# RMSNorm with repeated rows on one core: the second group's first load in two transfers

## The chip, the cores and the metric

The kernel runs on one core of one Trainium2 chip. The metric is the device time of one execution in microseconds (us); lower is better. The time before is the median of three runs.

## The reference

```
x: (8, 512, 2048) float32     gamma: (2048,) float32
x_rep  = repeat(x, 2, axis=1)                       # each row twice: (8, 1024, 2048)
rms    = sqrt(mean(x_rep ** 2, over the last axis) + 1e-6)
out    = x_rep / rms * gamma                        # float32
```

Each of the 4,096 input rows of 8 KB is normalized, multiplied by gamma and written out twice. The input has 33.6 MB and the output 67.1 MB; there is no matrix product.

## The kernel before

One tile `y` in SBUF holds 24 rows of 2048 numbers in each of the 128 partitions, as three areas of eight rows: `first` (rows 0 to 7), `second` (8 to 15) and `third` (16 to 23). The input is cut into four loads of 8.39 MB. Each brings eight rows to each partition, 64 KB that lie together in DRAM. The output is cut into eight stores of 8.39 MB: four rows of each partition, each row twice.

The schedule is written out by hand (`manual_schedule`): every engine carries out its instructions in the order of the program, and waits by semaphores only for the data or the space that it needs. The function `four` does two loads and four stores, and it is called twice, so there are two groups. All eight-row loads (line 50) and all stores (line 53) are issued by SP on one DMA queue (q1 in the profile). The small loads of gamma are issued by ScalarE on its queue (q10).

In a group the order is as follows.

1. Load n goes to rows 4 to 11 (`first + K`): the upper half of `first` and the lower half of `second`. Load n + 1 goes to `third`. In the first group the constants come between the two: gamma, its broadcast to all partitions by GpSimd, and epsilon.
2. For load n's rows 0 to 3, two at a time: ScalarE sums the squares of each row (line 63) and takes the root (line 67). VectorE takes the reciprocal (line 73) and multiplies each row by it and by gamma (line 75) into every second row of `first`. ScalarE and VectorE copy those rows to the places beside them (line 82), and store (n, 0) sends `first`.
3. The same for load n's rows 4 to 7 within `second`, and store (n, 1).
4. ScalarE sums the squares of the eight rows of load n + 1. Its first four rows are scaled from `third` into `first`, which needs store (n, 0) to have read it; they are copied, and store (n + 1, 0) sends them. The last four are spread within `third`, and store (n + 1, 1) sends them.

The second group's first load, load 2, needs rows 4 to 11 free. Of these, rows 4 to 7 are read by store (1, 0) and rows 8 to 11 by store (0, 1). Its second load, load 3, needs `third` free, which store (1, 1) reads. On SP the order of issue is: load 0, load 1, stores (0, 0), (0, 1), (1, 0), (1, 1), load 2, load 3, stores (2, 0), (2, 1), (3, 0), (3, 1).

Gamma comes in one DMA with G = 16 pieces of C = 125 numbers, and in E = 3 more of 16 numbers each; GpSimd spreads the two parts by two broadcasts (lines 132 and 136). The pieces are staged in rows 0 to 2 of `y` in partition 0.

Of the kernel before, what the change touches and what calls it, by code (L numbers as in the profile page):

```python
# [1 line left out]

# [4 lines left out]


@with_exitstack
def kernel(  # L10
    ctx: ExitStack,
    tc: tile.TileContext,
    x: bass.AP,
    gamma: bass.AP,
    out: bass.AP,
):
    nc = tc.nc
    P = nc.NUM_PARTITIONS
    f32 = mybir.dt.float32
    Act = mybir.ActivationFunctionType  # L20
    Alu = mybir.AluOpType

    B, S, D = x.shape
    Bo, So, Do = out.shape
    R = So // S
    assert R == 2 and D == Do and B == Bo and So == S * R
    eps = 1e-6
    inv_d = 1.0 / float(D)


    K = 4
    N = B * S
    ntiles = N // (P * K)
    assert N % (P * K) == 0 and ntiles == 8
    H = 2
    x_t = x.rearrange("b s d -> (b s) d").rearrange("(n p k) d -> n p k d", p=P, k=H * K)
    out_t = out.rearrange("b s d -> (b s) d").rearrange("(n p h j) d -> n h p (j d)", p=P, h=H, j=K * R)

    singles = ctx.enter_context(tc.tile_pool(name="singles", bufs=1))
    rows = ctx.enter_context(tc.tile_pool(name="rows", bufs=1))  # L40
    junk = ctx.enter_context(tc.tile_pool(name="junk", bufs=1, space=bass.MemoryType.PSUM))
    small = ctx.enter_context(tc.tile_pool(name="small", bufs=4))

    y = rows.tile([P, 3 * K * R, D], f32, name="y")
    first, second, third = 0, K * R, 2 * K * R

    def load(n, at):
        nc.sync.dma_start(out=y[:, at : at + H * K, :], in_=x_t[n])  # L50

    def store(n, h, to):
        nc.sync.dma_start(
            out=out_t[n, h], in_=y[:, to : to + K * R, :].rearrange("p j d -> p (j d)")
        )

    def squares(at, rows):

        n = len(rows)
        ss = small.tile([P, n], f32, name=f"ss{n}")  # L60
        for c, k in enumerate(rows):
            sq = junk.tile([P, D], f32, name="sq")
            nc.scalar.activation(  # L63
                out=sq[:], in_=y[:, at + k, :], func=Act.Square, accum_out=ss[:, c : c + 1]
            )
        rms = small.tile([P, n], f32, name=f"rms{n}")
        nc.scalar.activation(out=rms[:], in_=ss[:], func=Act.Sqrt, scale=inv_d, bias=eps_t[:])  # L67
        return rms

    def scale(at, to, rows, rms):  # L70
        n = len(rows)
        rstd = small.tile([P, n], f32, name=f"rstd{n}")
        nc.vector.reciprocal(out=rstd[:], in_=rms[:])  # L73
        for c, k in enumerate(rows):
            nc.vector.scalar_tensor_tensor(  # L75
                out=y[:, to + R * k, :], in0=y[:, at + k, :], scalar=rstd[:, c : c + 1],
                in1=gamma_b[:], op0=Alu.mult, op1=Alu.mult,
            )

    def repeat(to, k0, k1, copy):  # L80
        y_r = y[:, to + R * k0 : to + R * k1, :].rearrange("p (k r) d -> p k r d", r=R)
        copy(out=y_r[:, :, 1, :], in_=y_r[:, :, 0, :])  # L82

    ctx.enter_context(tc.manual_schedule())

    half = K // 2
    up, down = list(range(K)), list(range(K - 1, -1, -1))

    def four(n, constants, step):


        load(n, first + K)
        constants()
        load(n + 1, third)
        for rows in (up[:half], up[half:]):
            scale(first + K, first, rows, squares(first + K, rows))
        repeat(first, 0, half, nc.scalar.copy)
        repeat(first, half, K, nc.vector.tensor_copy)
        store(n, 0, first)
        scale(second, second, down, squares(second, down))  # L100
        repeat(second, half, K, nc.scalar.copy)
        for k in range(0, half, step):
            repeat(second, k, k + step, nc.vector.tensor_copy)
        store(n, 1, second)
        roots = [squares(third + h * K, up) for h in range(H)]
        scale(third, first, up, roots[0])
        repeat(first, 0, half, nc.scalar.copy)
        repeat(first, half, K, nc.scalar.copy)
        store(n + 1, 0, first)
        scale(third + K, third, up, roots[1])  # L110
        repeat(third, 0, K, nc.scalar.copy)
        store(n + 1, 1, third)

    gamma_b = singles.tile([P, D], f32, name="gamma_b")
    G, E = 16, 3
    C = D // G - E
    gamma_s = y[0:1, 0:2, :].rearrange("p k (c d) -> p (k c) d", c=G // 2)
    gamma_t = y[0:1, 2, :]
    eps_t = singles.tile([P, 1], f32, name="eps_t")

    def constants():
        nc.scalar.dma_start(
            out=gamma_s[0:1, :, :C],
            in_=gamma[: G * C].rearrange("(p c d) -> p c d", p=1, c=G),
        )
        for c in range(E):
            at = G * C + c * G
            nc.scalar.dma_start(
                out=gamma_t[0:1, c * G : (c + 1) * G],
                in_=gamma[at : at + G].partition_broadcast(1),  # L130
            )
        nc.gpsimd.partition_broadcast(  # L132
            out_ap=gamma_b[:, : G * C].rearrange("p (c d) -> p c d", c=G),
            in_ap=gamma_s[0:1, :, :C],
        )
        nc.gpsimd.partition_broadcast(out_ap=gamma_b[:, G * C :], in_ap=gamma_t[0:1, : E * G])  # L136
        nc.vector.memset(eps_t, eps)  # L137

        root = singles.tile([P, 1], f32, name="root")[:]
        nc.scalar.activation(out=root, in_=eps_t[:], func=Act.Sqrt)  # L140

    four(0, constants, half)
    four(2, lambda: None, 1)


# [1 line left out]
_INS = ['x', 'gamma']  # L147
_OUTS = [((8, 1024, 2048), 'float32')]


# [23 lines left out]
```

## Time and profile before

| | |
|---|---|
| median of 3 runs | 238.07 us (238.01 to 238.34) |
| profiled execution | 238.07 us, span 236.2 us |
| busy: ScalarE / VectorE / GpSimd | 110.2 / 84.5 / 2.8 us |
| HBM read / written | 33.56 / 67.11 MB, 426 GB/s over the span |
| ScalarE idle until a load landed | 70.4 us in two waits |
| a row's sum of squares (line 63, ScalarE) | 1878 ns |
| a row's scaling (line 75, VectorE) | 2349 ns |
| SP's issue of a load (line 50) | 340 to 425 ns |
| issue to landing: loads / stores (median) | 31.4 / 24.8 us |

The span runs from the first to the last instruction; the rest of the time lies around it. Times in the profile are counted from the span's start. A wait "A <- B" is idle time of A that B's end released. The DMA row has the mean busy share of the 16 DMA engines in each fortieth of the span, in tenths. The queue lines give packets, MB, and the share of the 16 engines' time that the packets took. In the chain of work, the columns are start, duration, and what filled it.

### The profile page before, as it was taken

How to read it: one execution, taken by the hardware profiler on the slowest of the kernel's cores; microseconds unless marked ns; L12 is line 12 of the kernel's file. 1: busy time of each engine (PE TensorE's matmuls, PEld its weight loads, DVE VectorE, ACT ScalarE, POOL GpSimd, SP SyncE). 2: the span in 40 equal slices, each digit the busy share in tenths (PEclk: the TensorE clock that was granted, in tenths of full speed). 3: DMA queues.
4: the chain of work that ended last, by engine and by line, in shares of the span. 5: the costliest groups of instructions: out<-in, count | busy, mean ns of one | idle time of the engine just before them, and what ended most of it. 6: DMA issues, size and time to landing. Idle time of an engine off the chain costs nothing.

```text
span 236.2 us, 226 instructions
## 1 busy us (share of the span) xinstructions
DVE 84.5 (36%) x48; ACT 110.2 (47%) x86; POOL 2.8 (1%) x6
## 2 busy tenths in 40 slices
DVE  0000396594699500000000007928919992000000
ACT  2001989479998470000000049991999957400000
POOL 0110000000000000000000000000000000000000
DMA  9898989989898989989898998989898998989894
GB/s 355 356 533 355 510 377 422 466 366 522 355 533 356 533 355 422 466 377 510 355 533 355 488 400 355 533 355 533 355 533 355 488 399 355 533 355 533 355 533 178
DMA packets 1767, 100.68 MB, mean 426 GB/s; under 512 B 230, under 2 KB 230, under 8 KB 230
## 3 DMA queue, kind: packets, MB, share of 16 engines
q1 hardware_dynamic: 1728, 100.66, 98.7%
q10 hardware_dynamic: 38, 0.01, 0.0%
q14 instruction: 1, 0.01, 0.0%
HBM read 33.56 MB, written 67.11 MB: 426 GB/s over the span
## 4 chain that ended last, share of the span: by engine, by line
DMA 45%; ACT 26%; DVE 12%; issue 2%; DVEq 0%
DMA y<-in_x_dram 26%; DMA out_dram<-y 20%; ACT sq L63 15%; DVE y L75 12%; ACT y L82 11%; ACT rms L67 1%; DVE rstd L73 0%; DVEq L75 0%
## 5 line engine op out<-in xcount | busy, mean ns | idle before, releaser
L63 ACT ACTIVATE sq<-y 128x2048 f32<-128x2048 f32 x32 | 60.1, 1878 | 71.1 <-DMA y<-in_x_dram 70.4
L75 DVE SCALAR_TENSOR_TENSOR y<-y,rstd,gamma_b 128x2048 f32<-128x2048 f32 x32 | 73.8, 2349 | 1.6 <-DMA out_dram<-y 1.0
L82 ACT COPY y<-y 128x4096 f32<-128x4096 f32 (+1 forms) x10 | 42.6, 4283 | 19.1 <-DVE y L75 18.3
L73 DVE RECIPROCAL rstd<-rms 128x4 f32<-128x4 f32 (+1 forms) x10 | 1.7, 170 | 109.2 <-ACT rms L67 109.2
L82 DVE COPY y<-y 128x4096 f32<-128x4096 f32 (+1 forms) x5 | 9.2, 1865 | 0.1
L63 ACT ACTIVATION_READ_ACCUMULATOR sq<-y 128x1 f32 x32 | 6.0, 186 | 0.0
L67 ACT ACTIVATE rms<-ss,eps_t 128x4 f32<-128x4 f32 (+1 forms) x10 | 3.0, 297 | 0.3
L140 ACT ACT_TABLE_LOAD x1 | 1.3, 1283 | 2.6 <-issue 2.6
L132 POOL PARTITION_BROADCAST gamma_b<-y x1 | 2.2, 2243 | 10.2 <-DMA y<-in_gamma_dram 10.2
L136 POOL PARTITION_BROADCAST gamma_b<-y x1 | 0.3, 323 | 10.1 <-DMA y<-in_gamma_dram 10.1
L137 DVE MEMSET eps_t<- 128x1 f32 x1 | 0.1, 59 | 0.8 <-PEq L158 0.8
L140 ACT ACTIVATE root<-eps_t 128x1 f32<-128x1 f32 x1 | 0.2, 203 | 0.0
L158 POOL MEMSET const-bfloat16-1.0<- 128x1 bf16 x1 | 0.1, 102 | 0.0
L158 POOL MEMSET const-float32-0.0<- 128x1 f32 x1 | 0.1, 99 | 0.2 <-issue 0.2
L158 POOL MEMSET const-uint8-127<- 128x1 uint8 x1 | 0.1, 101 | 0.0
L158 POOL MEMSET const-float32-1.0<- 128x1 f32 x1 | 0.1, 98 | 0.0
## 6 DMA issues: line engine op xcount, KB each, us to landing
out_dram<-y SPq DMA_DIRECT2D x8, 24.8
y<-in_x_dram SPq DMA_DIRECT2D x4, 31.4
y<-in_gamma_dram ACTq DMA_DIRECT2D x3, 0.1 KB
y<-in_gamma_dram ACTq DMA_DIRECT2D x1, 7.8 KB, 9.8
```

What stands on the lines that cost most here:

```text
L63: nc.scalar.activation(out=sq[:], in_=y[:, at + k, :], func=Act.Square, accum_out=ss[:, c : c + 1])
L67: nc.scalar.activation(out=rms[:], in_=ss[:], func=Act.Sqrt, scale=inv_d, bias=eps_t[:])
L73: nc.vector.reciprocal(out=rstd[:], in_=rms[:])
L75: nc.vector.scalar_tensor_tensor(out=y[:, to + R * k, :], in0=y[:, at + k, :], scalar=rstd[:, c : c + 1], in1=gamma_b[:], op0=Alu.mult, op ...
L82: copy(out=y_r[:, :, 1, :], in_=y_r[:, :, 0, :])
L132: nc.gpsimd.partition_broadcast(out_ap=gamma_b[:, : G * C].rearrange("p (c d) -> p c d", c=G), in_ap=gamma_s[0:1, :, :C],)
L136: nc.gpsimd.partition_broadcast(out_ap=gamma_b[:, G * C :], in_ap=gamma_t[0:1, : E * G])
L137: nc.vector.memset(eps_t, eps)
L140: nc.scalar.activation(out=root, in_=eps_t[:], func=Act.Sqrt)
L158: nc = _bacc.Bacc("TRN2", target_bir_lowering=False, num_devices=1)
```

## The change

`load` gets a number of parts and issues one DMA for each, cut along the rows of each partition. `four` passes it on for its first load: the first group has one part as before, and the second group has H = 2. Load 2 so becomes two DMAs of 4.19 MB, rows 0 to 3 and 4 to 7 of each partition, 32 KB that lie together in DRAM for each. Gamma comes as 16 pieces of 126 numbers and two DMAs of 16 numbers instead of three.

```
-    def load(n, at):
-        nc.sync.dma_start(out=y[:, at : at + H * K, :], in_=x_t[n])
+    def load(n, at, parts=1):
+        w = H * K // parts
+        for k in range(0, H * K, w):
+            nc.sync.dma_start(out=y[:, at + k : at + k + w, :], in_=x_t[n][:, k : k + w, :])
...
-    def four(n, constants, step):
+    def four(n, constants, step, parts):
...
-        load(n, first + K)
+        load(n, first + K, parts)
...
-    G, E = 16, 3
+    G, E = 16, 2
...
-    four(0, constants, half)
-    four(2, lambda: None, 1)
+    four(0, constants, half, 1)
+    four(2, lambda: None, 1, H)
```

## The prediction

> **What bounds the kernel now.** I began with the page, because its share of DMA time says whether any engine can matter at all.
>
> ```profile
> span 236.2 us, 226 instructions
> ...
> DVE 84.5 (36%) x48; ACT 110.2 (47%) x86; POOL 2.8 (1%) x6
> ...
> DMA  9898989989898989989898998989898998989894
> ...
> q1 hardware_dynamic: 1728, 100.66, 98.7%
> ...
> DMA 45%; ACT 26%; DVE 12%; issue 2%; DVEq 0%
> ```
>
> The loads and stores all go through SP's queue (q1), and its packets fill 98.7% of the time of the 16 DMA engines. No slice of the span has a hole. VectorE and ScalarE are busy 36% and 47%. The chain (last line) puts 38% on ACT and DVE all the same. It runs from wait to wait, and does not know that a store issued after a computation then stands behind other transfers. So I set the chain in order of time beside SP's own waits.
>
> ```profile
> 76.17 23.86 DMA out_dram<-y
> 100.03 0.02 issue
> 100.04 38.78 DMA y<-in_x_dram
> 138.82 0.02 issue
> 138.85 2.01 ACT sq L63 x2
> ```
>
> ```profile
> SPq L53 <- DVE y L82: 84.1, 4, 35.2
> SPq L53 <- ACT y L82: 60.9, 4, 19.9
> SPq L50 <- DMA out_dram<-y: 31.9, 2, 19.3
> ```
>
> The second group's first load (load 2) is issued at 100.04 us and lands after 38.78 us. One transfer of 8.39 MB fills the engines for only some 19.3 us, so half of the 38.78 us is queueing behind the store ahead of it. To see whether the queue ever runs dry I read the trace's single DMA packet records (start, duration, size). Each of the 12 transfers is 128 packets of 64 KB, eight on each engine: 1,536 in all, of which 1,367 took 2.418 us, and the next begins 2.414 us after the one before. From the first packet of a transfer to the first of the next it is 19.318 or 19.319 us in 8 of 11 cases, which is 8 x 2.414 plus 0.007 for the semaphore write. The other three are 19.917 (the opening load), 19.354, and 19.739 (the last store of group one to load 2).
>
> So the profiled time adds up thus: the first packet starts at 1.74 us; 12 x 19.319 = 231.83; extra 1.43 (0.60 in the opening load, 0.42 at the turn from store to load, 0.04, and the rest the engines' offset from each other); last packet ends at 235.0; 1.2 to the end of the span; 1.87 around it. That is 238.07, and the median of the three runs is 238.07 too, so nothing needs rescaling. Only 1.43 us of the whole isn't bytes at full rate.
>
> The tightest point for computation is the first store of group two:
>
> ```profile
> 152.94 2.29 DVE L82 COPY y<-y 128x4096 f32<-128x4096 f32 x1
> ...
> 155.30 48.29 SPq L53 DMA_DIRECT2D out_dram<-y  x4
> ```
>
> It is issued at 155.30 us, when the copy at line 82 is done. Its first packet starts at 157.34, right behind load 3's, with no gap. The opening load needed 1.02 us from issue (0.72) to first packet (1.74), so this store had 157.34 - 155.30 - 1.02 = 1.0 us to spare. Small, but positive: no time is lost there.
>
> **The change part by part.**
>
> *The split of load 2, what it moves.* The first half fills y rows 4 to 7, which store (1, 0) reads, so it waits for the same landing as before and is issued at 100.04. The second half fills rows 8 to 11, free since store (0, 1) landed long before, and follows at once. Half a transfer is 9.66 us, so the first half lands at about 138.8 - 9.7 = 129.1 instead of 138.8. The squares, scaling and copies of rows 0 to 3 need nothing else and move up by 9.7 us. ScalarE reaches row 4 at 151.6 - 9.7 = 141.9, after the second half has landed (138.9): no new wait. It finishes the second four rows' copy at 168.4 - 9.7 = 158.7, and load 3 lands at 158.2, so that isn't waited for either. The first store is issued at 145.6 instead of 155.3. Its spare time grows from 1.0 to 10.7 us, and its packets still start at 157.3, because the queue is in order and load 3 stands ahead. Gain on the path: 0. The stall doesn't vanish but goes on: the scaling into `first` for load 3's rows has to wait until that store has read them, at 177.53 now:
>
> ```profile
> 155.30 22.23 DMA out_dram<-y
> 177.53 0.03 issue
> 177.56 0.05 DVEq L75
> 177.61 0.04 issue
> 177.65 7.62 DVE y L75 x4
> ```
>
> That moment is set by the queue and stays. From there the last two stores are issued where they were, or up to 3 us earlier for the third (ScalarE is free sooner), and those already had cover: the fourth's issue is at 203.3 and its packets start at 215.3.
>
> *The split, what it adds on SP.* One DMA instruction, 0.34 us by its row (340 to 425 ns at line 50). Behind it on SP stands load 3, which waits for the landing of store (1, 1) at 119.7; SP is idle from 100.4 to then, so it costs 0. Without that cover load 3 would be issued 0.34 us later, and it has until 138.0 before its packets' turn. Nobody waits for the added instruction but the rows of the second half, and those are 9.7 us off. POOL's and ACT's queues are not passed.
>
> *The split, what it adds on the DMA engines, which is the path.* Each engine carries 16 packets of 32 KB instead of 8 of 64 KB, and one more semaphore write. No row has 32 KB. The nearest are 64 KB at 2.418 us and the 8 KB instruction fetch in mid run at 0.309 us: the slope is 2.109 us over 57,344 bytes, and what remains at zero bytes is 0.008 us per packet. Eight more packets are 0.06 us, with the semaphore write 0.07. Low end: the records overlap by 4 ns, so 8 x 0.004 + 0.007 = 0.04; below nothing only if the turn from store to load (0.42) shrinks with smaller first packets, which would give -0.35. High end: the slowest 8 KB fetch, ahead of the program, took 0.512 us, 0.21 over its bytes; 8 x 0.21 = 1.7 us. I take 0.05, since 32 KB back to back in one queue is nearest to the 64 KB row and to the fetch in mid run.
>
> *Does a new transfer have a start-up of its own?* The trace has one load directly behind another, at 21 us: the boundary shows no stretched packet on any engine, and at the full queue's other boundaries the price is 0.007 us. The Trainium skill's "DMA: Bandwidth & Descriptors" (section "Anatomy of one DMA") gives a fixed cost of about 2 us for each DMA, most of it the wait for the write's receipt; if that were paid in line here, the estimate would be 240.1 us. The same page's "Rules for kernel authors" says that transfers under way together share the same 16 engines and serialize, so that splitting one (over partitions, in its wording) is not worth it. The first figure doesn't fit the 0.007 us of the boundaries, where the receipt is waited for beside the next transfer's bytes.
>
> *Gamma.* One issue on ACT's queue (213 to 671 ns) and two small packets (data and semaphore, 11 and 9 ns on one engine) go; the main piece has rows of 504 B instead of 500. ScalarE then idles until 22.67 us in any case. The second broadcast at line 136 ends at 23.3, some 2 to 5 us earlier with one small DMA less in line, and VectorE first needs gamma_b at 27.3: covered by 4 us. Worth at most 0.02 us on one engine: 0.
>
> Sum: 238.07 + 0.05 = 238.12 us.
>
> **The rivals.**
>
> *The halves don't chain (slower).* The second half starts as the opening load did, whose first packets took 2.83 to 3.52 us in place of 2.418, some 0.8 more in the mean. Place: the engines at about 128 us. Time: 238.07 + 0.05 + 0.8 = 238.9. For it: load 2 already lies behind the one costly turn (0.42). Against: the two loads at 21 us chain without it. It decides from a gap of 0.43 us on.
>
> *Small packets are dear (slower).* At the high end above, 239.8; it passes 0.2% from 0.054 us a packet on. Against: 8 KB in 0.309 us leaves 0.008.
>
> *Work done earlier fills holes (faster).* If all 1.43 us that aren't bytes went, 236.6. But they lie at the opening and at 118 us, ahead of every instruction that moves. Only the 0.42 can be touched: 237.7, still within the bound. More than that would need the first store to starve in some runs, and in the profiled one it has 1.0 us.
>
> *The change doesn't take hold.* The squares wait for both halves (one wait for the whole buffer). Then ScalarE starts at 138.9 as now, and the time is 238.1 by the same DMA sum.
>
> **How the numbers follow.** 0.2% of 238.07 is 0.48 us, about what a measurement of this kernel tells from no change (its three runs lie 0.33 apart). Forecast, 238.12: 0.70; not taking hold, also no change: 0.10. Halves not chaining: 0.08; dear packets: 0.06. Faster by over 0.48: 0.06. So faster 0.06, same 0.80, slower 0.14. The range goes from 237.7 (the turn's 0.42 saved) to 238.7, which takes in a boundary gap of 0.6 us and leaves out the dear packets.
>
> **What would show it.** Right: q1 with 1872 packets (144 more), the chain's first group-two square at about 129.2, SP's first group-two store issued near 145.6, q1's share still at 98% or more, and first packets of successive stores 19.319 us apart. Wrong: a gap or stretched packets at about 128 us; 32 KB packets over 1.27 us; VectorE's resumption not at 177.6; or ScalarE still starting at 138.9 (taking hold). The forecast fails if the engines' full rate depends on the packets' size or order, which the trace has only for 64 KB.

## The result and the profile after

The change makes the kernel slower: 239.38 us (median of 6, 239.2 to 239.53) against 238.09 us (median of 6, 238.0 to 238.98) for the kernel before. The ratio is 1.0045, 95% interval 1.0031 to 1.0058. The prediction was 238.12 us, "same" with a chance of 0.80, and its range ended at 238.7.

The profiled execution took 239.53 us, with a span of 237.7. The page of the changed kernel, in the lines that answer to those shown before:

```profile
span 237.7 us, 225 instructions
...
DVE 84.5 (36%) x48; ACT 110.5 (47%) x86; POOL 2.8 (1%) x6
...
DMA  9898989899998989898999999899898989899994
...
q1 hardware_dynamic: 1872, 100.66, 98.5%
```

The page shows almost nothing. The queue is as full as before and has the 144 extra packets of the split; the engines' busy times are the same. A share of 98.5% of a longer span does not say that the packets ran at full rate: a stretched packet counts as busy. The chain of work in order of time shows where the two executions part:

```profile
100.12 29.39 DMA y<-in_x_dram
129.51 0.02 issue
129.53 2.01 ACT sq L65 x2
...
145.99 32.95 DMA out_dram<-y
178.93 0.03 issue
178.96 0.05 DVEq L77
179.01 0.04 issue
179.06 0.18 DVE y L77
```

The first half of load 2 lands at 129.5 us and the first store of group two is issued at 145.99, both as planned (129.2 and 145.6). But that store lands at 178.93 instead of 177.53, and VectorE, which waits for it, resumes at 179.06 instead of 177.65. The forecast had named this moment as one that stays. So by then the DMA engines had lost 1.4 us, and single packets show where.

The DMA view of a window of 6 us (154 to 160) cuts it into 40 slices of 0.15 us; in so narrow a window the row marks the slices in which packets begin. Before the change:

```profile
DMA  0000009990000000000000999000000000000099
...
DMA packets 60, 2.88 MB, mean 481 GB/s; under 512 B 16, under 2 KB 16, under 8 KB 16
```

After:

```profile
DMA  0000009990090000000000000099999990090000
...
DMA packets 48, 2.10 MB, mean 350 GB/s; under 512 B 16, under 2 KB 16, under 8 KB 16
```

The first marks in both rows, from 154.9 us, are the last packets of load 3, the eighth on each engine. Before, the store's first packets begin 16 slices on, at 157.3. After, they begin at 158.0 to 159.3, spread out and late. The trace's single packet records give the size: load 3's last packets took 2.77 to 3.61 us on all 16 engines in place of 2.418 (2.418 to 2.427 before). All earlier packets of load 3 were at full rate, save for the one engine that an instruction fetch held up.

In what follows, "lost" is the time from the start of one packet to the start of the next on the same engine, over the 2.414 us of a packet at full rate (1.2095 for 32 KB), as a mean over the 16 engines. The changed kernel lost 0.84 us there, the kernel before 0.01. The sum over the whole execution, as mean of the engines' last packet ends: 235.72 us against 234.81, so 0.91 later. Of that, 0.83 lies at load 3's end, 0.07 at the turn before load 2 (0.25 against 0.18), 0.08 in and around the 32 KB packets, and -0.07 in the opening and small items. The last engine lost more than the mean (1.11 at load 3's end and 0.42 in its first 32 KB packet) and ends at 236.54 against 235.01: that is the 1.5 us of the two profiled times.

### The profile page after: what moved, and what is told of

Same layout as the page of the kernel before. It is cut to its first block, busy times and chain, and to the rows that moved or that the text cites. A ratio compares the mean times of both kernels' runs of the same rounds, so it can differ in the third digit from the quotient of the medians.

```text
span 237.7 us, 225 instructions
## 1 busy us (share of the span) xinstructions
DVE 84.5 (36%) x48; ACT 110.5 (47%) x86; POOL 2.8 (1%) x6
## 3 DMA queue, kind: packets, MB, share of 16 engines
q1 hardware_dynamic: 1872, 100.66, 98.5%
## 4 chain that ended last, share of the span: by engine, by line
DMA 45%; ACT 26%; DVE 12%; issue 2%; DVEq 0%; SPq 0%
DMA out_dram<-y 24%; DMA y<-in_x_dram 22%; ACT sq L65 15%; DVE y L77 12%; ACT y L84 10%; ACT rms L69 1%; DVE rstd L75 0%; DVEq L77 0%; SPq L52 0%
```

## The experiments

Theory A: a store that the queue knows well before the load ahead of it has finished stretches that load's last packets. Rivals: gamma or the semaphores' order (G), the computation that now runs beside load 3 (B), the 32 KB packets and the state in which they leave the engines (C). Each time is compared with runs of the kernel before on the same chip (238.07 to 238.4 us there). Issue means the first store of group two.

| kernel | issue, us | lost at load 3's end | time, us | ratio (95%) |
|---|---|---|---|---|
| before | 155.30 | 0.01 | 238.09 | 1 |
| changed | 145.99 | 0.84 | 239.38 | 1.0045 (1.0031 to 1.0058) |
| gamma_only | 155.62 | 0.03 | 238.50 | 1.0011 (1.0002 to 1.002) |
| split_only | 145.66 | 0.90 | 239.36 | 1.0045 (1.0031 to 1.0059) |
| hold_two | 155.17 | 0.05 | 238.54 | 1.002 (1.001 to 1.003) |
| hold_scalar | 153.86 | 0.81 | 239.72 | 1.0061 (1.0049 to 1.0073) |
| hold_four | 152.82 | 0.77 | 239.24 | 1.0046 (1.0034 to 1.0059) |
| whole_early | 139.12 | 0.81 | 239.59 | 1.0058 (1.0045 to 1.007) |
| both_groups | 146.51 | 0.05 | 239.38 | 1.0049 (1.0036 to 1.0062) |
| both_drained | 149.37 | 1.49 | 244.11 | 1.0245 (1.0228 to 1.0261) |
| late_load | 155.71 | 0.01 | 238.42 | 1.0007 (0.9998 to 1.0016) |

**One part at a time.** First gamma's part alone:

```
-    G, E = 16, 3
+    G, E = 16, 2
```

> Gamma's part of the change alone, load 2 in one transfer. Theory A (the early store: a store that stands in the queue before the last packets of the load ahead of it run stretches those packets): no store is issued earlier, so 238.1 us, and load 3's last packets keep 2.418 us. Rival G (gamma's staging or the semaphores' order costs it): 239.4 us.

Then the split alone, with `G, E = 16, 3` back in the changed kernel:

> The split of load 2 alone; gamma as before, in one large and three small DMAs. Theory A: the store of group two is as early as in the changed kernel, and the time is 239.2 to 239.5 us, so that gamma has no part in it. If gamma or the order of semaphores has: 238.3 to 238.9 us.

The split alone has the whole effect (1.0045 both times). Gamma's part is at 1.0011, inside the 0.2% that the forecast called no change, and its load 3 lost nothing to speak of. Rival G falls.

**The store held back, the rest left early.** In the changed kernel's second group the copy of rows 2 and 3 is moved behind the first scaling of rows 4 to 7 on VectorE:

```
-        repeat(first, half, K, nc.vector.tensor_copy)
-        store(n, 0, first)
...
+            for c, k in enumerate(down):
+                if c == 1:
+                    repeat(first, half, K, nc.vector.tensor_copy)
+                    store(n, 0, first)
+                nc.vector.scalar_tensor_tensor(
...
```

> The whole change, but the copy of rows 2 and 3 on VectorE, which the first store of group two waits for, comes after the first scaling of rows 4 to 7. The squares and scalings are as early as in the changed kernel; the store is issued at about 155.7 us of the span instead of 146.0 (155.3 before the change). Theory A: load 3's last packets are back at 2.42 us and the time is 238.1 to 238.2 us. Rival B (the computation that now runs beside load 3's end stretches its packets): 239.4 us. Rival C (the two transfers of 32 KB packets leave the engines in a worse state for what follows): 239.4 us.

The timeline of this kernel around the issue:

```profile
141.88 1.88 ACT L65 ACTIVATE sq<-y 128x2048 f32<-128x2048 f32 x1
...
152.82 2.29 DVE L84 COPY y<-y 128x4096 f32<-128x4096 f32 x1
155.02 6.99 DVE L113 SCALAR_TENSOR_TENSOR y<-y,rstd,gamma_b 128x2048 f32<-128x2048 f32 x3
155.17 9.65 SPq L55 DMA_DIRECT2D out_dram<-y  x2
157.40 3.60 ACT L84 COPY y<-y 128x4096 f32<-128x4096 f32 x1 [7.10 <-DVE y L113]
```

The squares of rows 4 to 7 begin at 141.88 instead of 151.61, so the computation is as early as in the changed kernel, VectorE is at work right through load 3's end, and the 32 KB packets are all there. Only the store's issue is back at 155.17. The loss falls from 0.84 to 0.05 us and the time from 1.0045 to 1.002. This speaks against B and C. The remaining 0.2% is not all explained: 0.05 us are the split, and the engine that ends last is the one that carried an instruction fetch (it lost 0.31 us in each of two packets); gamma_only, which has no split, is already at 1.0011.

With `if c == 0` in place of `c == 1` the store goes out some 2.3 us earlier:

> As the run before, with the copy ahead of all four scalings of rows 4 to 7, so that the store is issued at about 153.3 us. Load 3's last packet on an engine starts at 155 to 156 us. Theory A, if what counts is that the store's first packet is known before the last load packet starts (issue plus 1.0 us): stretched as in the changed kernel, 239.2 to 239.4 us. If the lead has to be longer than that: 238.1 us. Rivals B and C: 239.4 us.

```profile
152.82 51.88 SPq L55 DMA_DIRECT2D out_dram<-y  x4
```

The store's issue at 152.82 brought the loss back: 0.77 us, and 1.0046. The DMA rows of the window from 154 to 160 us show both runs, with the issue at 155.17 first and at 152.82 below:

```profile
DMA  0000009990090000000000999090900000000099
DMA  0000009999900000000000000099999909000000
```

In the first, the store's packets begin at 157.3 us, as before the change; in the second, at 157.9 and later. The two kernels differ in nothing but the place of this copy and store in the order.

And with the copy on ScalarE, behind the squares of rows 4 to 7, it goes out between the two:

```
...
+        rms = squares(second, down)
+        if parts > 1:
+            repeat(first, half, K, nc.scalar.copy)
+            store(n, 0, first)
+        scale(second, second, down, rms)
```

> The whole change, but rows 2 and 3 are copied by ScalarE after the squares of rows 4 to 7, so that the first store of group two is issued at about 154.3 us, between the run at 152.8 (stretched on every engine, 0.77 us in the mean) and that at 155.2 (0.05). Load 3's last packets start between 154.95 and 155.7 us, engine by engine, and the store's descriptors should be there at 155.3 (issue plus 1.0). Theory A: engines whose last packet has begun before that lose nothing, the later ones 0.3 to 1.2 us, so 0.1 to 0.6 us in the mean and 238.5 to 239.2 us. If the lead must be a whole packet on every engine: 0.05 us and 238.5 us.

```profile
153.86 51.06 SPq L55 DMA_DIRECT2D out_dram<-y  x4
```

The issue came at 153.86, earlier than aimed at. If a store needs the 1.0 us that the opening load took from issue to first packet (an estimate), its descriptors were there at 154.9, just when the first of load 3's last packets began (154.91; the last engine's at 155.71), and all engines lost (0.33 to 1.3 us). At 155.17, so known at about 156.2 by the same estimate, every engine was already in its last packet, and the loss was 0.05. The edge therefore lies at an issue between 153.9 and 155.2, that is, known between 154.9 and 156.2, and the last load packets begin within that stretch. The time of this run (1.0061) is some 0.3 us above the changed kernel's, but its spans are not: 237.4 to 237.6 us against 237.3 to 237.7. The 0.3 us lie outside the span (2.2 us around it in place of 1.8 to 1.9), and why is not shown.

**The store early without the split.** The kernel before, whose second group leaves out the squares, scaling and copies of load 2's rows 0 to 3:

```
-        for rows in (up[:half], up[half:]):
-            scale(first + K, first, rows, squares(first + K, rows))
...
+        if n == 0:
+            for rows in (up[:half], up[half:]):
+                scale(first + K, first, rows, squares(first + K, rows))
...
         store(n, 0, first)
```

> The kernel before the change, load 2 in one transfer, gamma as before; group two leaves out the squares, scaling and copies of load 2's rows 0 to 3, so that its first store waits for load 2's landing alone and is issued at about 138.9 us. Theory A: load 3's last packets are stretched and the time is 239.3 to 239.6 us, without any 32 KB packet and with less computation. Rivals B and C: 238.1 us.

```profile
0.72 0.85 SPq L50 DMA_DIRECT2D y<-in_x_dram  x2
39.19 48.22 SPq L53 DMA_DIRECT2D out_dram<-y  x4
100.14 19.83 SPq L50 DMA_DIRECT2D y<-in_x_dram  x2
139.12 65.64 SPq L53 DMA_DIRECT2D out_dram<-y  x4
```

SP's part of the timeline shows the store going out at 139.12, as soon as load 2 has landed. There isn't one packet of 32 KB and there is less computation, and load 3's last packets lost 0.81 us. (Of the time's 1.0058, some 0.3 us lie outside the span here too.) With hold_two this settles what matters: the moment at which the store joins the queue.

**Is it paid at every turn?** Theory A as first put said so. The first group's first load was split as well:

```
-    four(0, constants, half, 1)
+    four(0, constants, half, H)
```

> The whole change, and the first group's first load in two transfers as well. Its first store is then ready some 9.7 us earlier, at about 29.5 us, ahead of load 1's last packets (38.6 us). Theory A (a store known to the queue before the last packets of the load ahead of it stretches them): a second turn is stretched, at 39 to 41 us, and the time grows by another 0.8 to 1.4 us, to 240.2 to 240.8 us. If the cost belongs to the split of load 2 or to the second group alone: 239.4 to 239.5 us.

```profile
29.51 58.94 SPq L55 DMA_DIRECT2D out_dram<-y  x4
101.05 20.03 SPq L52 DMA_DIRECT2D y<-in_x_dram  x3
146.51 58.21 SPq L55 DMA_DIRECT2D out_dram<-y  x4
```

A miss for theory A as put, and a telling one. Both first stores are early (29.51 and 146.51). The first turn, at load 1's end, lost 1.29 us; but the turn from store to load then lost 0.01 instead of 0.25, and load 3's end 0.05 instead of 0.84. The time is that of the changed kernel, which is what was expected if the cost belonged to the second group alone; the packets rule that out, since the loss now lies in the first group. Two kernels of transfers alone asked the same (`h` loads 4.19 MB, `s` stores 8.39 MB; both leave out all computation and gamma, and `s` sends what was loaded):

```
alternate:  h(0, A), h(1, A + K), h(2, B), s(A), h(3, B + K), s(A), h(4, C), s(B), h(5, C + K)
            s(B), h(6, A), s(C), h(7, A + K), s(C), s(A), s(A)
grouped:    h(0, A), h(1, A + K), h(2, B), h(3, B + K), h(4, C), h(5, C + K)
            s(A), s(A), s(B), s(B), h(6, A), h(7, A + K), s(C), s(C), s(A), s(A)
```

> Transfers alone: all computation and gamma are left out, the stores send what was loaded. Eight loads of 4.19 MB and eight stores of 8.39 MB, in an order with six turns from load to store and five from store to load, all known to the queue well ahead. Theory A: each turn from load to store costs 0.8 to 1.2 us and each back 0.2 to 0.6 us; against the next kernel, with two and one, 4.0 to 7.2 us more. If a turn costs nothing without computation beside it: the same time as the next kernel.

> The same transfers alone, the same sizes and count, in an order with two turns from load to store and one back. By the sum of the packets, 231.8 + 0.2 us, with the opening and the end about 236 us in the span without turns; theory A: 2 x 0.8 to 1.2 and 0.2 to 0.6 us more, 239 to 241 us in all.

They took 241.04 and 239.27 us, 1.8 apart where 4.0 to 7.2 were expected. In alternate the first turn from load to store lost 1.19 (over the last two packets of 32 KB), and the other five 0.03 to 0.14; the five turns back 0.01. In grouped it was 0.92 at the first turn and 0.03 at the second. Computation is not needed for the loss, and it is paid once. What sets alternate apart in the profiled run is mostly one engine, which lost 1.2 us at a later turn and ends 3.4 us after the earliest; why is not shown.

Once an execution, or once for as long as the queue doesn't run empty? In both_groups, load 2 was made to wait for the landing of store (1, 1):

```
+        if n:
+            nc.scalar.copy(out=y[:, third, :16], in_=y[:, 0, :16])
+            nc.scalar.copy(out=y[:, first + K, :16], in_=y[:, third, :16])
+            nc.scalar.copy(out=y[:, second, :16], in_=y[:, third, :16])
         load(n, first + K, parts)
```

> The kernel with both groups' first loads split, whose profile shows 1.29 us lost an engine at the first group's early turn from load to store and 0.05 at the second's, though that store is early too. Here load 2 is held until store (1, 1) has landed (three copies of 16 numbers on ScalarE make it wait), so that the queue runs empty once, at about 120.5 us. Theory A1 (the price is paid once for each stretch in which the queue doesn't run empty): the second turn, at 160 to 163 us, loses 0.8 to 1.3 us an engine again. Theory A2 (once an execution): 0.05 us again. The gap itself and load 2's new start-up should cost 2.5 to 3.5 us: in all 242 to 243 us under A2, 243 to 244.5 under A1.

```profile
29.62 58.89 SPq L55 DMA_DIRECT2D out_dram<-y  x4
120.94 1.29 SPq L52 DMA_DIRECT2D y<-in_x_dram  x3
149.37 60.04 SPq L55 DMA_DIRECT2D out_dram<-y  x4
```

Load 2 is issued at 120.94 us, when the engines have nothing left, and starts up like the opening load (0.54 lost on its first packets). The second turn then lost 1.49 us, where it had lost 0.05 without the gap. So the price is not paid once an execution; it comes back after the queue has run empty. One thing is not told apart: load 2 was also late here, so that no early turn from store to load stood ahead of the second store. Whether a late load alone brings the price back, without an empty queue, no run shows.

**The other turn.** The kernel before also has one early turn, from store (1, 1) to load 2, with 0.18 lost on the store's last packets. Load 2 was held back to 116.72 by copies on the idle ScalarE, whose values it overwrites:

```
+        if n:
+            for a, b, w in ((0, K, K), (0, K, K), (0, K, 1)):
+                nc.scalar.copy(out=y[:, b : b + w, :], in_=y[:, a : a + w, :])
+            nc.scalar.copy(out=y[:, K, :512], in_=y[:, 0, :512])
         load(n, first + K)
```

> The kernel before the change, with load 2 held back: after store (1, 0) has landed, ScalarE, which is idle there, copies rows 0 to 3 over rows 4 to 7 twice and a little more (values that load 2 overwrites), which takes some 16.6 us, so that load 2 is issued at about 116.7 us instead of 100.0. If the turn from store to load is dear for the same reason as the one from load to store (theory A for both directions), the last packets of store (1, 1) are back at 2.418 us and the time falls by 0.2 to 0.4 us, to 237.9 us. If the 0.42 us at that turn is a load's own start-up (its first packets then take up to 1.1 us more, as at the opening), the time stays at 238.1 to 238.3 us or grows by up to 0.7 us.

```profile
116.72 3.03 SPq L50 DMA_DIRECT2D y<-in_x_dram  x2
```

The store's last packets were back at 2.418 us, and load 2's first packets lost 0.29 in their place: 1.0007 (0.9998 to 1.0016), no gain. A load that comes late shows its own start-up. No version that was run beats the kernel before.

## Why the prediction was wrong

**The step that failed** is the one on the moved store: "Its spare time grows from 1.0 to 10.7 us, and its packets still start at 157.3, because the queue is in order and load 3 stands ahead. Gain on the path: 0." The order held, and the gain was indeed 0. But the step took it that an earlier issue can only help or do nothing, and so costed the earlier entry into the queue at 0. It cost 0.84 us in the mean of the engines and 1.1 on the last one. The sum of the packet records in the prediction had the hint: of 11 boundaries, eight were at 19.318 or 19.319 us, and one of the three exceptions, 19.739, was the only one where a transfer of the other direction had been known well ahead. I put it down to a turn from store to load, which the change leaves alone, and did not ask why the two turns from load to store were free. They were free because both stores came late: 39.20 and 155.30 us, some 1.8 and 2.0 us before their packets. So the 1.0 us of spare time, which I took for a margin against a starving queue, was small enough by luck to spare the kernel the loss. The 0.42 that the sum charged to the turn is the distance of the first packets; in the mean of the engines it is 0.18.

**The terms that held.** The split on the engines: load 2 took 9.685 + 9.682 = 19.367 us from first packet to first packet, 0.048 over 19.319; 0.05 was forecast, and 32 KB packets took 1.213 us. The second half chains onto the first without a gap, so the rival "the halves don't chain" fell, and "small packets are dear" with it. The Trainium skill's fixed cost of about 2 us a DMA ("DMA: Bandwidth & Descriptors", section "Anatomy of one DMA"), which the prediction set against this, is given there for DMAs that GpSimd issues, which the prediction left out; for these, issued by SP, it is not paid in line: the added boundary has the 0.007 us of the others. ScalarE's start (129.53 for 129.2), the store's issue (145.99 for 145.6), the 1,872 packets and the 98.5% came as told. ScalarE waits 0.41 us for load 3, which it was not to do; load 3 lands late, and nothing hangs on it. The last store, told as issued where it was, goes out at 204.66 instead of 203.26, since VectorE resumes later, and is still early. The second issue on SP took 1.24 us instead of 0.34; SP had nothing else to do. "The change doesn't take hold" fell too.

**The rivals.** The slower side had 0.14, on two mechanisms that both failed. The true one stood nowhere: that a store queued earlier slows the load ahead of it. The sentence on what would make the forecast fail ("if the engines' full rate depends on the packets' size or order") came near, but the order did not change; the time at which the order is known did.

**What stays open** is why. The Trainium skill's "DMA: Bandwidth & Descriptors" (section "Two DMAs through the same engine are not ordered") says that an engine's descriptors start in order but are pipelined, and that its read and write sides are separate queues. An engine could then read the store's data from SBUF while the last load packet is still being written there, and so run ahead once by a lead that it keeps until its queue is empty. That would fit a loss that comes at the first early turn, not at later ones, and again after a gap. It is only argued: the packet records here have one start and one duration, and no run shows the two sides apart.

## What to carry to other kernels

In a kernel whose DMA queue is full throughout, do not count an earlier issue as free: look at the last packets of the transfer ahead, above all where loads turn to stores, and compare turns whose next transfer was known early with turns where it came just in time. Work that is ready sooner gains nothing behind a full in-order queue, and it can lose about 1 us once. Judge such a queue by the duration of single packets, since the busy share counts a stretched packet as work.

## What the runs showed of the hardware

- On one hardware queue, a store known before the last packets of the load ahead begin stretches those packets by 0.33 to 1.8 us on each engine (0.77 to 0.90 in the mean of the engines where an early turn from store to load had come before, 0.92 to 1.49 where none had). A store issued 1.5 to 2.2 us before its first packet cost 0.01 to 0.05.
- Later turns lose 0.01 to 0.14 us in the mean, as long as the queue doesn't run empty. After a gap, with a late load behind it, the price is paid again (1.49 us).
- A boundary between transfers of one direction costs 0.007 us, also for halves of 4.19 MB.
- A load that follows a store late loses some 0.3 us in its first packets; known early, it takes about 0.2 from the store's last ones (0.01 where an early turn from load to store had come before).
- The 16 engines drift apart by 0.4 to 1.3 us (in one kernel 3.4), and the last one sets the time; an 8 KB instruction fetch in mid run costs the engine that it hits 0.3 to 0.6 us.
